# Division by the squared key length: from the keys of an RWKV-7 scan into the blocks of its inverse

## The chip, the cores and the metric

The kernel runs on one core of one Trainium2 chip. The metric is the device time of one execution in microseconds (us), as the median of several runs. A profile comes from one execution of its own, with its own time. The engines are called by their names in the profile: PE (TensorE, matrix products; PEld are its weight loads), DVE (VectorE), ACT (ScalarE), POOL (GpSimd), and SP (SyncE, which here issues the DMAs).

## The reference

The model is a trunk of two layers, with 1024 tokens, a width of 1024, and one final norm. Each layer normalizes its input, makes one combined projection, feeds three token mixers of width 512 (trailing means, retention, RWKV-7), gates and merges their outputs, and projects back. The change touches only the RWKV-7 mixer, which has 8 heads of 64 channels:

```
kk = heads(k * k_k)
kk = kk / max(sqrt(sum(kk * kk, axis=-1)), 1e-12)
k  = k * (1 + (a - 1) * k_a)
a_t, b_t = -kk, kk * a          # per head and token

def step(S, (r_t, w_t, k_t, v_t, a_t, b_t)):
    sa = einsum('bhvk,bhk->bhv', S, a_t)
    S  = S * w_t + sa (x) b_t + v_t (x) k_t
    return S, einsum('bhvk,bhk->bhv', S, r_t)
```

Both a_t and b_t carry the unit vector kk, and they only ever meet as a pair. One may therefore leave both of them unscaled and divide once, by the squared length of the key, anywhere on the way from sa to its use: it is one number for each token and head.

## The kernel before, in words

**The scan in chunks.** The tokens are cut into 16 chunks of 64. A head pair (two heads, 128 channels on 128 partitions) is worked on at a time, four pairs in a layer. Inside a chunk, the values sa of the 64 tokens depend on each other through a strictly triangular 64x64 matrix, so the kernel inverts (1 - triangle) for all 16 chunks and both heads at once, and then walks through the chunks with matrix products alone. For a head pair the steps are these:

- `prepare(h)` (line 1469), for each half h of 512 tokens: decay sums `Lc`, the squared keys `ksq`, split in two parts `ksh` and `ksl` so that a product with the block matrix `bone` sums them over a head's 64 channels in full precision (`nps`, lines 1490 to 1492). VectorE takes the maximum with 1e-24 (1494) and the reciprocal in two pieces of 256 (1495 to 1497): `rn` is one over the squared length, with the number of a token repeated on all 64 partitions of its head. Line 1507 multiplies key, k_k and rn, line 1509 multiplies with (a + 1), and lines 1518 to 1522 with the decay: `BK` holds the scaled b and k side by side.
- `place` (1541) writes the other operand, r and the unscaled key with their decay, into `AR`.
- `scores(q)` (1556): TensorE multiplies BK with AR for four chunks at a time, VectorE masks the products into `G`, which lies in the large tile `GX`.
- `invert()` (1603): of each 64x64 triangle, two 32x32 diagonal blocks are inverted on VectorE. A transpose brings them into `Lo` so that one partition holds one whole block in its 1024 elements, 64 partitions in all (two blocks, two heads, 16 chunks), and ScalarE copies `Lo` to `M` (1610). A recurrence of 30 steps follows (1614 to 1624), each of two VectorE instructions: an outer product of a column of Lo and a row of M into `RX`, and its sum into M. Line 1625 sets the diagonal to one. `back(b)` transposes block b into G, and `blocks` (1582) makes the off-diagonal block with 32x32 products on TensorE.
- `values(q)` (1641) prepares values, transposed keys (`BKt`) and the products `AV` that do not depend on the state.
- `main()` (1723): for each chunk, TensorE, VectorE (`xst`), TensorE (`ch`), ScalarE (`Z`), TensorE, VectorE (`S`, the new state) follow each other. Columns of the BKt tile beyond its 15 chunks hold `pc`, the decay over a chunk.

Pair hp + 1 is prepared, scored and inverted beside the scan of pair hp (`overlap`, `further`, lines 1795 to 1807). The pairs share the three slots of G (`SLOT`, 1438): the second half of a pair's scores waits for the first half of the chunks of the pair before.

**What fills TensorE beside it.** Large projections are made of 128x512 products in three passes (high and low halves of 32-bit numbers). A projection tile of 128 output channels takes 96 of them in the direct form (`in_tile2`, 2196). `SEQUENCE` (99) says which tiles are made in that form during a layer's scan: the k, r and v of head pairs 1 to 3, and a number g of branch gates in between. What is left comes afterwards in pairs, in a Strassen-like form that saves one product of eight (`forms`).

**What sets the order.** The program does not write an engine's order out by hand. A recorder (`Log`) collects all operations; `plan` (431) is a list scheduler that walks through modelled time with a cost for each instruction (`times`, 386), a cost and a landing time for each DMA, and a key for each operation (its place in the program and a bias of its lane), and sorts all five queues. Small two-operand subtractions on GpSimd may be moved to VectorE by it. Line 673 emits everything; it is therefore the line of almost every instruction in the profile, and groups are told apart by the names of their tiles. On the chip each queue then runs strictly in this order. A wait of the first instruction in a queue holds everything behind it.

Of the kernel before, what the change touches and what calls it, by code (L numbers as in the profile page):

```python
# [9 lines left out]
F32 = mybir.dt.float32  # L10
# [3 lines left out]
ALU = mybir.AluOpType  # L14
# [3 lines left out]
P = 128  # L18
D = 1024
T = 1024  # L20
L = 2
W = 512
HF = 512
# [72 lines left out]
COLUMNS = (1,)  # L96
TWICE = (1, 2)
SPARE = ((3, 2), (3, 3))
SEQUENCE = ('k1 r1 v1 g3 k2 r2 v2 g4 k3 g1 r3 v3 g12', 'k1 r1 v1 g3 k2 r2 v2 g4 k3 g1 r3 v3 g12')


ORDER = ("PE", "DVE", "ACT", "POOL", "SP")
# [584 lines left out]
def trunk_kernel(ctx, tc, xT, cvec, pos, vecs, consts, w_ada, w_all, pool_w, lora_w, out):  # L687
    nc = Log(tc.nc, tc)
# [125 lines left out]
    def vv(l, k, i):  # L814
        o = VEC[k] + i
        return vec[l][:, o : o + 1]
# [123 lines left out]
            yield 6000  # L940

    xd = [dp.tile([8, 2, P, HF], F32, name=f"xd{l}") for l in range(1)]
    gd = dp.tile([3, 8, 2, P, HF], F32, name="gd")
    hd = [dp.tile([8, 2, P, HF], F32, name=f"hd{l}") for l in range(L)]
    od = [dp.tile([3, 4, 2, P, HF], F32, name=f"od{l}") for l in range(L)]
# [75 lines left out]
    def pace(limit=900.0):  # L1021
        settle()
        return max(0.0, idle_at["DVE"] - clock[0] - limit)
# [416 lines left out]
    def rwkv_task(l, hp, kT, rT, vp, lt):  # L1440
# [12 lines left out]
        qa = lambda b: slice(64 + 32 * b, 96 + 32 * b)  # L1453
        BKt = BKt.rearrange("p (c n) -> p c n", n=P)
        Z = Z.rearrange("p (c n) -> p c n", n=P)
        pc = scan[l][1][:, 15 * P + 16 * hp : 15 * P + 16 * hp + 16]
        c3 = lambda t: t.rearrange("p (c t) -> p c t", t=CH)
        rm = cs("rmask", P).unsqueeze(1).to_broadcast([P, 4, P])
# [10 lines left out]
        def prepare(h):  # L1469
            if h == 0:  # L1470
                lw.append(lora_load(l, hp))
            yield wait(*lt[h])
            pss = [mx("lw"), mx("lw")]
            sg, aT = t_ri("sg"), t_ri("aT")
            lora_mm(pss, lw[0], lt[h], (sg, aT))
            nc.scalar.activation(sg, pss[0], AF.Tanh, bias=vv(l, "w0", hp), scale=0.5)
            yield 400
            nc.scalar.activation(aT, pss[1], AF.Tanh, bias=vv(l, "a0", hp), scale=0.5)
            sq = t_ri("ksq")
            nc.scalar.activation(sq, kT[h], AF.Square, scale=vv(l, "k_k", hp))  # L1480
            sqh = t_ri("ksh", F32R)
            nc.scalar.copy(sqh, sq)
            sql = t_ri("ksl", F32R)
            nc.vector.tensor_tensor(sql, sq, sqh.bitcast(F32), op=ALU.subtract)
            Lc = t_ri("Lc")
            nc.scalar.activation(sg, sg, AF.Identity, bias=ones)
            yield wait(sg)
            nc.vector.tensor_tensor_scan(Lc, same, sg, 0.0, op0=ALU.mult, op1=ALU.add)
            yield wait(sqh, sql, spare=1000)
            nps = mx("nps")  # L1490
            mmul(nps, bone, sqh, start=True, stop=False)
            mmul(nps, bone, sql, start=False, stop=True)
            rn = t_ri("rn")
            nc.vector.tensor_scalar_max(rn, nps, 1e-24)
            for j in range(2):
                yield pace()
                nc.vector.reciprocal(rn[:, 256 * j : 256 * j + 256], rn[:, 256 * j : 256 * j + 256])
            yield wait(Lc)
            Ep = sg
            nc.scalar.activation(Ep, Lc, AF.Exp, scale=-0.5 * KAPPA)  # L1500
            nc.scalar.activation(Lc, Lc, AF.Exp, scale=0.5 * KAPPA)
            Em = Lc
            kkn = rn
            ka = t_ri("ka")
            nc.scalar.activation(ka, aT, AF.Identity, bias=oka[l][:, hp : hp + 1], scale=vv(l, "k_a", hp))
            yield pace()
            nc.vector.scalar_tensor_tensor(kkn, kT[h], vv(l, "k_k", hp), rn, op0=ALU.mult, op1=ALU.mult)
            yield pace()
            nc.vector.scalar_tensor_tensor(kkn, aT, 1.0, kkn, op0=ALU.add, op1=ALU.mult)
            yield pace()  # L1510
            nc.vector.tensor_tensor(ka, ka, kT[h], op=ALU.mult)
            Ep_.append(Ep)
            for q in range(2):
                whole = t_ri("BK")
                b = whole.rearrange("p (c j t) -> p c j t", j=2, t=CH)
                part = slice(4 * q, 4 * q + 4)
                yield pace()
                nc.vector.scalar_tensor_tensor(
                    b[:, :, 0, :], c3(kkn)[:, part, :], -0.5, c3(Em)[:, part, :], op0=ALU.mult, op1=ALU.mult
                )  # L1520
                nc.vector.tensor_tensor(b[:, :, 1, :], c3(ka)[:, part, :], c3(Em)[:, part, :], op=ALU.mult)
                BK.append(whole)
            rk = ka
            yield pace()
            nc.vector.scalar_tensor_tensor(rk, rT[h], vv(l, "r_k", hp), ka, op0=ALU.mult, op1=ALU.mult)
            yield wait(rk)
            rkh = t_ri("rkh", F32R)
            nc.scalar.copy(rkh, rk)
            rkl = t_ri("rkl", F32R)
            nc.gpsimd.tensor_tensor(rkl, rk, rkh.bitcast(F32), op=ALU.subtract)  # L1530
            yield wait(rkh, rkl, spare=500)
            ps = mx("bon")
            bv = t_ri("bv")
            nc.touch(mmul(ps, bone, rkh, start=True, stop=False), bv)
            mmul(ps, bone, rkl, start=False, stop=True)
            nc.vector.scalar_tensor_tensor(bv, ps, 0.5, vp[h], op0=ALU.mult, op1=ALU.mult)
            bvs.append(bv)
            if h:
                prepared.add((l, hp))
# [36 lines left out]
        def back(b):  # L1576
            q = slice(32 * b, 32 * b + 32)
            src = M[q, :]
            src = src.rearrange("p (t s) -> p t s", s=32) if hi_ - lo_ == 1 else src.rearrange("p (t h s) -> p t h s", h=2, s=16)
            nc.vector.transpose(out=pair_(q, qa(b)), in_=src)  # L1580

        def blocks(*parts):
            tiles = [mx("m1") for _ in parts]
            with nc.together():
                for u in range(16):
                    for (i, q), ps in zip(parts, tiles):
                        rows = slice(32 - 32 * i, 64 - 32 * i)
                        w = 16 * q + u
                        g = 16 * (hi_ if q else lo_) + u
                        mmul(  # L1590
                            ps[rows, u * 32 : u * 32 + 32],
                            Lo[32:64, w * 32 : w * 32 + 32] if i else G[0:32, g, 96:128],
                            G[32:64, g, 96:128] if i else T13[:, w, :],
                            timed=True,
                        )
            for (i, q), ps in zip(parts, tiles):
                g = 16 * (hi_ if q else lo_)
                if i:
                    nc.scalar.copy(G[0:32, g : g + 16, 96:128], ps[0:32, :].rearrange("p (u s) -> p u s", s=32))
                else:  # L1600
                    nc.scalar.copy(Lo[32:64, q * HF : (q + 1) * HF], ps[32:64, :])

        def invert():
            for b in range(2):
                q = slice(32 * b, 32 * b + 32)
                yield pace()
                dst = Lo[q, :]
                dst = dst.rearrange("p (t s) -> p t s", s=32)
                nc.vector.transpose(out=dst, in_=pair_(q, qa(b)))
                nc.scalar.copy(M[q, :], Lo[q, :])  # L1610
            yield wait(MT)
            M3, L3 = (x.rearrange("p (t s) -> p t s", s=32) for x in (M, Lo))
            tm = RX[0:64, :]
            for i in range(1, 31):
                n = 31 - i
                pr = tm[:, 0 : n * i].rearrange("p (t s) -> p t s", s=i)
                nc.vector.tensor_tensor(
                    pr,
                    L3[:, i + 1 :, i : i + 1].to_broadcast([64, n, i]),
                    M3[:, i : i + 1, 0:i].to_broadcast([64, n, i]),  # L1620
                    op=ALU.mult,
                )
                nc.vector.tensor_tensor(M3[:, i + 1 :, 0:i], M3[:, i + 1 :, 0:i], pr, op=ALU.add)
                yield pace(600)
            nc.vector.memset(M[:, 0:1024:33], 1.0)
            nc.vector.transpose(
                out=T13.rearrange("p u s -> p s u"), in_=M[0:32, :].rearrange("p (t s) -> p s t", s=32)
            )
            yield pace()
            back(1)  # L1630
            yield pace()
            blocks((0, 0))
            yield 500
            back(0)
            yield 1500
            blocks((0, 1), (1, 0))
            yield 1500
            blocks((1, 1))
            yield wait(GX)

        def values(q):
# [1178 lines left out]
```

## Time and profile before

| | |
|---|---|
| median of 3 runs | 2245.52 us (2244.77 to 2245.91) |
| the profiled execution: its time, its span from first to last instruction | 2244.16 us, 2242.4 us |
| granted PE clock, mean | 0.997 |
| instructions of the program | 34866 |
| DMA | 247.79 MB, 111 GB/s on average |

An instruction group in the profile reads: line, engine, operation, tile written <- tiles read, shape and type, xcount, then busy us and mean ns, then the engine's idle time ahead of it, and what ended that. A tile row gives durations as min/median/max in ns, and the first and last start in us. A wait row gives who waited for whom, the total in us, how often, and the longest. Matmul records overlap, because TensorE takes up the next product before the last one has left.

The first layer's scan lies between about 190 and 546 us, the second layer's between about 1287 and 1631 us.

### The profile page before, as it was taken

To read this page: it belongs to the slowest core of one execution; us is meant where nothing else is said; L and a number is where in the kernel's file an instruction comes from. 1 tells how busy PE (TensorE), PEld (TensorE's weight loads), DVE (VectorE), ACT (ScalarE), POOL (GpSimd) and SP (SyncE) were. 2 spreads that over 40 slices of the span, in tenths; PEclk is the share of its full clock that TensorE was granted. 3 is DMA by queue.
4 is the path that set the end of the run, shared out by engine and by line. 5 is a ranking of instruction groups with operands and counts; after the bars stand their busy time and mean duration, and the time that the engine had idled before them with its cause. 6 is when DMAs were issued, how large, how long until landed. Compare 5 with 4: busy or idle time off the path is not lost.

```text
span 2242.4 us, 34866 instructions
## 1 busy us (share of the span) xinstructions
PE 2204.3 (98%) x12740; PEld 1823.8 (81%) x12740; DVE 1730.7 (77%) x2904; ACT 995.3 (44%) x1933; POOL 727.5 (32%) x629
## 2 busy tenths in 40 slices
PE   7999999999999999999999999999999999999998
PEld 6778888887888888888878887888888888888887
DVE  6888868886889886669787879799466767665895
ACT  5644554445333334324465354554443343341254
POOL 2222223233555663320042122232153455341100
PEclk9999999999999999999999999999999999999999
DMA  8111112333433335754451212133232122357343
GB/s 318 62 55 55 55 62 77 124 104 109 123 114 109 104 115 176 241 178 137 134 166 31 67 35 62 53 110 107 81 105 63 62 68 63 108 188 230 113 141 113
DMA packets 139195, 247.79 MB, mean 111 GB/s; under 512 B 15760, under 2 KB 21136, under 8 KB 139024
## 3 DMA queue, kind: packets, MB, share of 16 engines
q1 hardware_dynamic: 139024, 245.56, 34.7%
q8 instruction: 101, 1.65, 0.3%
q14 instruction: 70, 0.57, 0.1%
HBM read 185.99 MB, written 59.51 MB: 109 GB/s over the span
## 4 chain that ended last, share of the span: by engine, by line
PE 88%; DVE 6%; ACT 2%; DMA 1%; issue 1%; POOL 0%; SPq 0%; DVEq 0%; ACTq 0%; POOLq 0%
PE acc L673 73%; PE two L673 3%; PE ch L673 2%; PE g L673 1%; PE m L673 1%; PE ro L673 1%; PE av L673 1%; DVE rn L673 1%; DVE MT L673 1%; DVE RX L673 1%; PE pps L673 1%; PE rs L673 1%; PE bt L673 1%; PE lw L673 1%; PE rkv L673 0%
## 5 line engine op out<-in xcount | busy, mean ns | idle before, releaser
L673 PE MATMUL acc<-hlo,wh 128*128 128x512 f32 x1328 | 533.5, 402 | 0.0
L673 PE MATMUL acc<-hhi,wl 128*128 128x512 f32 x1328 | 532.7, 401 | 0.0
L673 PE MATMUL acc<-hhi,wh 128*128 128x512 f32 x1328 | 530.8, 400 | 0.5 <-DVE k L673 0.4
L673 POOL TENSOR_TENSOR wl<-wr,wh 128x512 fp32r<-128x512 f32 x125 | 170.4, 1364 | 404.3 <-ACT wh L673 170.0
L673 PEld LDWEIGHTS acc<-hhi,wh 128*128 128x128 f32 x1328 | 250.2, 188 | 45.9 <-DVE k L673 0.9
L673 PEld LDWEIGHTS acc<-hlo,wh 128*128 128x128 f32 x1328 | 250.3, 188 | 43.5
L673 PEld LDWEIGHTS acc<-hhi,wl 128*128 128x128 f32 x1328 | 250.3, 189 | 42.7
L673 PE MATMUL acc<-T,wh 128*128 128x512 f32 x768 | 244.4, 394 | 0.0
L673 ACT CAST wh<-wr 128x512 fp32r<-128x512 f32 x194 | 119.5, 616 | 198.5 <-PE acc L673 151.7
L673 POOL TENSOR_TENSOR wl<-wsum,wh 128x512 fp32r<-128x512 f32 x90 | 124.6, 1385 | 165.4 <-ACT wh L673 126.7
L673 PEld LDWEIGHTS acc<-T,wh 128*128 128x128 f32 x768 | 143.8, 188 | 29.7
L673 PE MATMUL acc<-T,wl 128*128 128x512 f32 x384 | 151.6, 395 | 0.0
L673 ACT CAST wh<-wsum 128x512 fp32r<-128x512 f32 x128 | 79.3, 620 | 140.6 <-PE acc L673 131.3
L673 ACT CAST wh<-wraw 128x512 fp32r<-128x512 f32 x108 | 66.9, 619 | 127.5 <-PE acc L673 79.2
L673 POOL TENSOR_TENSOR wl<-wraw,wh 128x512 fp32r<-128x512 f32 x59 | 85.5, 1450 | 72.8 <-ACT wh L673 66.2
L673 DVE SCALAR_TENSOR_TENSOR S<-ch,BKt,SP 64x64 f32<-64x64 f32 x224 | 63.3, 282 | 58.9 <-PE ch L673 55.8
L673 DVE TENSOR_TENSOR RX<-MT 64x30 f32<-64x30 f32 (+14 forms) x240 | 88.9, 370 | 8.6 <-ACT MT L673 1.3
L673 ACT ACTIVATE SP<-S,BKt 128x128 f32<-128x128 f32 x112 | 45.0, 402 | 104.4 <-DVE S L673 103.7
L673 DVE TENSOR_TENSOR MT<-MT,RX 64x30 f32<-64x30 f32 (+14 forms) x240 | 85.0, 354 | 7.3
L673 ACT ACTIVATE gsg<-acc 128x512 f32<-128x512 f32 x88 | 52.4, 595 | 80.3 <-PE acc L673 79.9
L673 ACT COPY Z<-ch 64x128 f32<-64x128 f32 x128 | 33.1, 259 | 120.5 <-PE ch L673 119.9
L673 PEld LDWEIGHTS acc<-T,wl 128*128 128x128 f32 x384 | 72.1, 188 | 14.8
(378 smaller groups left out, 5095.7 us busy)
## 6 DMA issues: line engine op xcount, KB each, us to landing
wr<-in_w_all SPq DMA_DIRECT2D x214, 256.0 KB, 2.7
wraw<-in_w_all SPq DMA_DIRECT2D x144, 256.0 KB, 2.7
gd<-gsg SPq DMA_DIRECT2D x96, 256.0 KB, 2.0
gs<-gd SPq DMA_DIRECT2D x84, 256.0 KB, 3.5
wada<-in_w_ada SPq DMA_DIRECT2D x80, 256.0 KB, 2.8
ol<-od SPq DMA_DIRECT2D x48, 256.0 KB, 3.3
traw<-hd SPq DMA_DIRECT2D x28, 256.0 KB, 3.0
x<-in_xT SPq DMA_DIRECT2D x16, 256.0 KB, 4.8
```

Source lines behind the costliest of these rows:

```text
L673: o.inst = f(*map(self.fixed, a), **{q: self.fixed(v) for q, v in k.items()})
```

## The change

In `prepare`, the maximum, the two reciprocals and the product with rn are gone from the keys. ScalarE copies nps out of PSUM (`ns`). SyncE stores two rows of it (one for each head) to DRAM, `nd`, and loads it back in another layout: `RN`, 64 partitions (block, head, chunk) by 32 tokens, in free columns of the BKt tile. The one remaining product, (a + 1) times the key, writes over `aT`. The factor k_k, which the program holds with its sign turned, goes into the product with the decay, in the place of the constant -0.5.

In `invert`, the transposed blocks go straight into M, and the recurrence reads and writes M alone. RN becomes 1 / (-2 max(n, 1e-24)), with n the squared length. One product over 64x1024 multiplies row t of each block with the number of token t ahead of the recurrence; another one multiplies column s with the number of token s behind it, after the diagonal has been set to one. The order of `back` and `blocks` at the end changes: block (0, 0) comes ahead of back(1), back(0) comes last.

In `SEQUENCE`, the gate between k3 and r3 moves to the end: g1 and g12 become g13, in both layers.

```diff
-SEQUENCE = ('k1 r1 v1 g3 k2 r2 v2 g4 k3 g1 r3 v3 g12', 'k1 r1 v1 g3 k2 r2 v2 g4 k3 g1 r3 v3 g12')
+SEQUENCE = ('k1 r1 v1 g3 k2 r2 v2 g4 k3 r3 v3 g13', 'k1 r1 v1 g3 k2 r2 v2 g4 k3 r3 v3 g13')
...
+    nd = [dp.tile([4, 2, 2, HF], F32, name=f"nd{l}") for l in range(L)]
...
+        RN = scan[l][1][0:64, 15 * P + 64 + 32 * (hp % 2) : 15 * P + 96 + 32 * (hp % 2)]
...
-            rn = t_ri("rn")
-            nc.vector.tensor_scalar_max(rn, nps, 1e-24)
-            for j in range(2):
-                yield pace()
-                nc.vector.reciprocal(rn[:, 256 * j : 256 * j + 256], rn[:, 256 * j : 256 * j + 256])
+            ns = t_ri("ns")
+            nc.scalar.copy(ns, nps)
+            nc.sync.dma_start(out=nd[l][hp, h], in_=ns[0:P:64, :])
+            for b in range(2):
+                o = 32 * b + 16 * (own[h] == hi_)
+                nc.sync.dma_start(
+                    out=RN[o : o + 16, :],
+                    in_=nd[l][hp, h].rearrange("e (c b t) -> (e c) b t", b=2, t=32)[:, b, :],
+                )
...
-            kkn = rn
+            kkn = aT
...
-            nc.vector.scalar_tensor_tensor(kkn, kT[h], vv(l, "k_k", hp), rn, op0=ALU.mult, op1=ALU.mult)
-            yield pace()
-            nc.vector.scalar_tensor_tensor(kkn, aT, 1.0, kkn, op0=ALU.add, op1=ALU.mult)
+            nc.vector.scalar_tensor_tensor(kkn, aT, 1.0, kT[h], op0=ALU.add, op1=ALU.mult)
...
-                    b[:, :, 0, :], c3(kkn)[:, part, :], -0.5, c3(Em)[:, part, :], op0=ALU.mult, op1=ALU.mult
+                    b[:, :, 0, :], c3(kkn)[:, part, :], vv(l, "k_k", hp), c3(Em)[:, part, :], op0=ALU.mult, op1=ALU.mult
...
-                dst = Lo[q, :]
+                dst = M[q, :]
                 dst = dst.rearrange("p (t s) -> p t s", s=32)
                 nc.vector.transpose(out=dst, in_=pair_(q, qa(b)))
-                nc.scalar.copy(M[q, :], Lo[q, :])
+            nc.vector.tensor_scalar(RN, RN, 1e-24, -2.0, op0=ALU.max, op1=ALU.mult)
+            nc.vector.reciprocal(RN, RN)
             yield wait(MT)
-            M3, L3 = (x.rearrange("p (t s) -> p t s", s=32) for x in (M, Lo))
+            M3 = M.rearrange("p (t s) -> p t s", s=32)
             tm = RX[0:64, :]
+            nc.vector.tensor_tensor(M3, M3, RN.unsqueeze(2).to_broadcast([64, 32, 32]), op=ALU.mult)
...
-                    L3[:, i + 1 :, i : i + 1].to_broadcast([64, n, i]),
+                    M3[:, i + 1 :, i : i + 1].to_broadcast([64, n, i]),
...
             nc.vector.memset(M[:, 0:1024:33], 1.0)
+            nc.vector.tensor_tensor(M3, M3, RN.unsqueeze(1).to_broadcast([64, 32, 32]), op=ALU.mult)
...
             yield pace()
+            blocks((0, 0))
             back(1)
-            yield pace()
-            blocks((0, 0))
+            yield 1000
+            blocks((0, 1), (1, 0))
             yield 500
+            blocks((1, 1))
             back(0)
-            yield 1500
-            blocks((0, 1), (1, 0))
-            yield 1500
-            blocks((1, 1))
             yield wait(GX)
```

## The prediction

> **What bounds the kernel now.** I read the page's engine lines first, then its chain of waits.
>
> ```profile
> PE 2204.3 (98%) x12740; PEld 1823.8 (81%) x12740; DVE 1730.7 (77%) x2904; ACT 995.3 (44%) x1933; POOL 727.5 (32%) x629
> ...
> PE 88%; DVE 6%; ACT 2%; DMA 1%; issue 1%; POOL 0%; SPq 0%; DVEq 0%; ACTq 0%; POOLq 0%
> ```
>
> TensorE is busy 98% of the span and carries 88% of the chain that ended last; VectorE, the engine that the change relieves, carries 6%. A busy share alone proves little here, because matmul records overlap. So I looked for a stretch in which TensorE waits for nothing, and at the stages of the scan beside it (busy time by stretch).
>
> ```profile
> 874.43 238.69 PE acc L673 x1040
> ...
> 150.00:250.00 100.00, 99.97 (x717) 82.73 (x715) 84.94 (x173) 50.62 (x111) 23.16 (x23) 1.00 0.17 53
> 350.00:450.00 100.00, 99.28 (x759) 81.20 (x757) 86.74 (x173) 47.36 (x109) 29.75 (x30) 1.00 0.33 103
> 875.00:1115.00 240.00, 240.00 (x1051) 196.59 (x1051) 176.36 (x244) 87.55 (x150) 45.68 (x32) 1.00 0.54 171
> ```
>
> The piece of the chain at 874 us is 1040 matmuls in 238.69 us, so one 128x512 matmul costs 0.2295 us when nothing holds it. The columns of the stretches are TensorE, weight loads, VectorE, ScalarE, GpSimd, clock and DMA. In the scan (150 to 250, 350 to 450) VectorE is busy 85% to 87%, yet TensorE is idle for at most 0.7 us in those 100. By weight loads, which do not overlap each other, the pure stretch stands at 196.59/240 = 81.9% and the whole span at 1823.8/2242.4 = 81.3%: what the program could still gain on TensorE, lead-in and end included, is some 0.7%, 16 us. The Trainium skill ("Perfetto Trace Analysis", Identifying the Most-Contended Engine) says that busy share is no measure for TensorE and that the share of weight loads should be used; the trace agrees, and adds that 82%, not 100%, is the ceiling here.
>
> What TensorE still waits for between 75 and 2200 us stands in the waits by engine (total us, times, longest):
>
> ```profile
> PE two L673 <- ACT y L673: 1.8, 1, 1.8
> PE acc L673 <- DVE r L673: 1.3, 1, 1.3
> PE two L673 <- DVE S L673: 1.2, 3, 0.6
> ...
> PE m L673 <- DVE MT L673: 0.9, 1, 0.9
> ...
> PEld ch L673 <- DVE xst L673: 7.4, 23, 0.5
> ```
>
> These are the waits that a lighter VectorE could shorten. The row on xst is the weight loads' idle time, most of which lies under a matmul that is still streaming; that is why it does not appear among TensorE's own waits.
>
> The last question is whether the scan's end sets the length of a layer's first stage. First and last starts of the gate evacuations and of the state update, first layer, then second:
>
> ```profile
> L673 ACT ACTIVATE gsg<-acc x40: 570/598/601, 154.5 to 562.5; 128x512 f32<-128x512 f32 x40
> ...
> L673 DVE SCALAR_TENSOR_TENSOR S<-ch,BKt,SP x112: 265/284/292, 194.8 to 545.1; 64x64 f32<-64x64 f32 x112
> ...
> L673 ACT ACTIVATE gsg<-acc x40: 577/598/602, 1253.5 to 1660.7; 128x512 f32<-128x512 f32 x40
> ...
> L673 DVE SCALAR_TENSOR_TENSOR S<-ch,BKt,SP x112: 265/284/292, 1292.0 to 1629.9; 64x64 f32<-64x64 f32 x112
> ```
>
> The state update ends 17.4 us and 30.8 us before the last gate. The recurrence is not late: TensorE's big products are. A scan that ends sooner buys nothing by itself.
>
> **The change, part by part.** *TensorE.* The matmuls are the same in number and shape. The sequence takes 3+4+1+12 = 20 gates now and 3+4+13 = 20 after, so as many go through the direct products and as many through the paired ones. On the path: 0.
>
> *VectorE, preparation.* Sixteen halves (2 layers, 4 head pairs, 2 halves) each lose the maximum from PSUM, two reciprocals and one product.
>
> ```profile
> L673 DVE RECIPROCAL rn<-rn 128x256 f32<-128x256 f32 x32 | 55.6, 1742 | 0.5
> L673 DVE SCALAR_TENSOR_TENSOR rn<-k,vec,rn 128x512 f32<-128x512 f32 x16 | 11.6, 726 | 0.2
> L673 DVE TENSOR_SCALAR rn<-nps 128x512 f32<-128x512 f32 x16 | 10.9, 680 | 0.8 <-PE nps L673 0.6
> L673 DVE TENSOR_TENSOR mlo<-mrg,mhi 128x512 fp32r<-128x512 f32 x32 | 21.9, 684 | 0.0
> L673 DVE TENSOR_TENSOR BK<-ka,Lc 128x256 f32<-128x256 f32 x32 | 13.4, 418 | 0.2
> L673 DVE STREAM_TRANSPOSE GX<-MT 32x1024 f32<-32x1024 f32 x16 | 31.1, 1946 | 0.4
> ...
> L673 DVE RECIPROCAL rn<-rn x37: 165/1752/1754, 17.3 to 2234.9; 128x256 f32<-128x256 f32 x32, 128x4 f32<-128x4 f32 x3, 128x2 f32<-128x2 f32 x2
> ```
>
> Removed: 55.6 + 11.6 + 10.9 = 78.1 us, or 4.9 us a half. The product that is left now writes over aT, so it waits for ScalarE's read of aT; behind it stands only the product with ka, which needs that same ScalarE result, so this costs nothing.
>
> *VectorE, inverse.* Eight inverses each gain two products of 64x1024, a maximum and a reciprocal of 64x32. A product grows from 418 ns at 256 to 684 at 512, 1.04 ns an element, so 1024 cost 684 + 532 = 1.22 us. The trace has no 64x1024 product; its bounds are 0.68 (the 512 row, if a broadcast operand were free) and 1.37 (twice that row). The reciprocal lies between 0.165 (4 elements) and 1.742 (256), on their line at 0.34; the small maximum I put at 0.2. Together 2 x 1.22 + 0.54 = 3.0 us an inverse, 24 us in all. Net VectorE: -54 us of 1730.7, nearly all in the scan stages.
>
> *ScalarE.* It loses the copy of the transposed block and gains a copy out of PSUM.
>
> ```profile
> L673 ACT COPY MT<-MT 32x1024 f32<-32x1024 f32 x16 | 16.8, 1047 | 14.6 <-DVE MT L673 14.4
> ...
> L673 ACT COPY s<-acc 128x512 f32<-128x512 f32 x64 | 37.3, 582 | 10.0 <-PE acc L673 10.0
> ```
>
> That is -16.8 + 16 x 0.582 = -7.5 us on an engine at 44%. The PSUM bank of nps is now freed by ScalarE after 0.58 us instead of by VectorE after 0.68.
>
> *The chain of the inverse.* Gone is one ScalarE copy of 1.05 us ahead of the recurrence and the step back(1), a transpose of 1.95 us, ahead of the first block product; new are the 3.0 us. It is as long as before, within a microsecond either way. The blocks' products and back(0) only change order.
>
> *The DMAs and SyncE's queue.* Each half stores 4 KB and loads two pieces of 2 KB: 48 new issues. The loads must see the store's landing, and SyncE stands meanwhile.
>
> ```profile
> gd<-gsg SPq DMA_DIRECT2D x96, 256.0 KB, 2.0
> ...
> lraw<-in_lora_w SPq DMA_DIRECT2D x16, 64.0 KB, 2.1
> ...
> fixed<-in_cvec SPq DMA_DIRECT2D x1, 4.0 KB, 1.7
> ...
> SPq L673 <- POOL wl L673: 473.3, 120, 38.7
> ...
> SPq L673 <- DMA od<-wo: 22.2, 8, 3.9
> ...
> L673 DVE TENSOR_SCALAR rn<-nps x16: 659/679/692, 88.2 to 1489.0; 128x512 f32<-128x512 f32 x16
> ...
> L673 DVE MEMSET MT<- x8: 85/85/85, 150.8 to 1532.6; 64x32 f32 x8
> ```
>
> The number a token needs is there 0.6 (copy) + 2.0 (store) + 1.7 to 2.1 (load) = 4.3 to 4.7 us after nps. In the last head pair nps is read at 1489.0 and the recurrence begins by 1532.6: 43.6 us of cover, of which the shorter preparation may take 10. What queues behind the waiting SyncE are the weight loads; a store followed by its load holds it 22.2/8 = 2.8 us in the program now, so 16 times that is 45 us, spread over both scans. SyncE stands 473 us for the weight halves' buffers anyway. I take 0; without that cover it would be up to 2.8 us a time. The Trainium skill speaks against this step ("DMA: Bandwidth & Descriptors", Two DMAs through the same engine are not ordered): the issuing engine must wait for the first DMA's semaphore before it issues the second. The row on od shows just such a wait, 2.8 us on average.
>
> *The sequence.* One gate, 96 x 0.2295 = 22.0 us of TensorE, moves from before r3 to after v3. The last pair's preparation starts 22 us earlier, beside the scan of pair 2, and the gate lands where nothing else waits. On the path: 0, unless the collision below happens.
>
> **The sum.** What is left for TensorE to gain are waits. At least none go (0); at most the rows r, S, MT and the weight loads on xst all go, 1.3 + 1.2 + 0.9 + 7.4 = 10.8 us. I take TensorE's own rows, 3.4 us, because they are time in which nothing streamed. ScalarE's 1.8 stays: nothing in the change touches it. New waits can cost as much as old ones, so the end on the other side is +3.4. The profiled execution took 2244.16 us, 1.8 around a span of 2242.4; 2244.16 - 3.4 = 2240.8. The median of the runs lies 1.36 above that execution, so 2242 us.
>
> **The rivals.** *More comes free than the waits show* (2230 to 2237, say 2233): entering and leaving small matmuls also costs TensorE, and a calmer VectorE lets the planner group them better. The 16 us worked out above are the limit. Against it: lead-in and end are in those 16 us, and the number of scan steps stays.
>
> *The freed time is filled again* (2244 to 2247): the planner orders every queue anew by its own cost model and may move GpSimd subtractions to VectorE, so that the waits return at other places. For it: today's few waits are scattered, no step of the scan is systematically late.
>
> *The early preparation collides with the scan* (2250 to 2258, say 2254, slower). The moved gate brings pair 3's preparation into pair 2's scan, where VectorE was 87% busy, and one step shows what a burst in its queue does:
>
> ```profile
> 416.26 2.99 DVE L673 TENSOR_TENSOR traw<-traw,traw 128x512 f32<-128x512 f32 x3 [0.16 <-DMA traw<-hd]
> ...
> 419.89 0.46 PE L673 MATMUL two<-S,CX 128*128 128x128 f32 x2 [0.61 <-DVE S L673]
> ```
>
> Three subtractions ahead of S, and TensorE, whose order is fixed, stands for 0.61 us. Pairs 2 and 3 have 15 such steps each, in two layers 60. With 14 more of them late by 0.61 us the result is 8.5 us above my forecast, 2250.5; that is the point from which it decides, and 20 give 2254. Against it: the preparation is 4.9 us a half lighter.
>
> *The number comes late.* Should a weight load ahead of the store hold SyncE for its longest, 38.7 us, the 4.7 us no longer fit into 43.6 - 10, and VectorE stands at the head of the inverse: (38.7 + 4.7 - 33.6) = 9.8 us once, 2252 us.
>
> **How the numbers follow.** A measurement of this kernel can tell about 0.2% (4.5 us) from no change: below 2241.0 is faster, above 2250.0 slower. My forecast, 2237 to 2246, has 0.60, of which 0.24 lies below 2241. The gain beyond the waits has 0.13, the refilling 0.14, the collision 0.10, the late number 0.03. Faster: 0.24 + 0.13 = 0.37. Same: 0.36 + 0.14 = 0.50. Slower: 0.13. The range is 2235 to 2251: it takes in the forecast, the refilling, a third of the first rival and the edge of the collision. The forecast's own range is 2237 to 2246.
>
> **What would show it.** Right: VectorE busy near 1676 us, ScalarE near 988, TensorE's instructions still 12740 and its share still 98%; recurrence products no shorter; the first rows of the waits on S, MT and r smaller, none new above 2 us. The last state update should come before 545 us and 1630 us with the last gate where it was. A row "DVE RN <- DMA" of more than a microsecond would prove the late number, waits on S in steps of pairs 2 and 3 the collision. The forecast is wrong if the span moves by more than the waits add up to.

## The result, and the profile after

The changed kernel takes 2239.93 us, median of 11 runs (2238.61 to 2241.09), against 2245.07 us (2243.57 to 2246.70) for 11 runs of the kernel before on the same chip: ratio 0.9974 [0.9966, 0.9982], 5.1 us less. The forecast was 2242.0 us, 3.5 below the median it started from. The profiled execution after took 2240.18 us with a span of 2238.4, 4.0 less than before.

The page's engine lines and the shares of its chain, after:

```profile
PE 2200.3 (98%) x12740; PEld 1824.4 (82%) x12740; DVE 1676.6 (75%) x2877; ACT 980.6 (44%) x1931; POOL 720.0 (32%) x624
...
PE 85%; DVE 9%; ACT 2%; issue 1%; DMA 1%; POOL 1%; SPq 0%; DVEq 0%; POOLq 0%; ACTq 0%
```

VectorE lost 54.1 us of work, and the span lost 4.0. TensorE has the same 12740 matmuls, and it is idle for as long as before: 2242.4 - 2204.3 = 38.1 us then, 2238.4 - 2200.3 = 38.1 us now. So all of the 4.0 us have gone out of the time in which TensorE counts as busy; the same products stand closer together. VectorE's share of the chain rose from 6% to 9% while it works less: the chain is one path among several, and a share that moves by three points is no measure of what bounds.

The waits by engine between 75 and 2200 us, after:

```profile
PE two L673 <- DVE S L673: 1.6, 3, 1.1
PE pps L673 <- ACT pdh L673: 1.1, 2, 0.8
...
PE acc L673 <- DVE r L673: 0.6, 1, 0.6
...
PEld ch L673 <- DVE xst L673: 4.3, 14, 0.5
```

The rows on y (1.8) and MT (0.9) are gone, r went from 1.3 to 0.6, xst from 7.4 (23 times) to 4.3 (14 times). S rose from 1.2 to 1.6 and pps from 0.7 to 1.1. All listed rows of TensorE's own waits add up to 10.4 us before and 9.2 after.

The stage ends, first layer and then second (gate evacuations, state update), and the start of the second layer (ssps, first start):

```profile
L673 ACT ACTIVATE gsg<-acc x40: 577/598/603, 151.7 to 559.8; 128x512 f32<-128x512 f32 x40
...
L673 DVE SCALAR_TENSOR_TENSOR S<-ch,BKt,SP x112: 267/284/292, 181.5 to 540.9; 64x64 f32<-64x64 f32 x112
...
L673 PE MATMUL ssps<-fixed,ssum x32: 164/250/250, 1111.0 to 2228.2; 128*128 128x1 f32 x32
...
L673 ACT ACTIVATE gsg<-acc x40: 575/598/604, 1249.0 to 1654.4; 128x512 f32<-128x512 f32 x40
...
L673 DVE SCALAR_TENSOR_TENSOR S<-ch,BKt,SP x112: 267/284/292, 1277.5 to 1621.4; 64x64 f32<-64x64 f32 x112
```

The same row on ssps before:

```profile
L673 PE MATMUL ssps<-fixed,ssum x32: 164/250/250, 1113.0 to 2232.2; 128*128 128x1 f32 x32
```

So the span splits into four stages, here as in the table further down: to the last gate of layer 1 (562.5 before, 559.8 after), from there to ssps, the paired products (550.5, 551.2), from ssps to the last gate of layer 2 (547.7, 543.4), and the rest (581.7, 584.0). The two scan stages gave 2.7 + 4.3 = 7.0 us, the other two took 0.7 + 2.3 = 3.0 back. Inside the first, TensorE's idle time went from 21.4 to 22.4 us, inside the third from 5.0 to 3.0: in the first layer none of the gain is idle time, in the second about half.

Where in the scan stages? Busy time by stretch, before and then after (columns as in the prediction: TensorE, weight loads, VectorE, ScalarE, GpSimd, clock, DMA):

```profile
90.00:280.00 190.00, 189.11 (x1268) 155.22 (x1267) 165.11 (x312) 95.18 (x199) 45.62 (x49) 1.00 0.16 48
280.00:565.00 285.00, 281.99 (x2117) 232.20 (x2115) 223.63 (x447) 142.67 (x320) 88.41 (x79) 1.00 0.31 98
...
1200.00:1390.00 190.00, 188.59 (x1371) 154.59 (x1369) 163.65 (x308) 93.26 (x192) 40.74 (x43) 1.00 0.17 52
1390.00:1660.00 270.00, 268.99 (x1953) 222.35 (x1953) 195.34 (x393) 127.80 (x295) 86.98 (x79) 1.00 0.29 92
```

```profile
90.00:280.00 190.00, 188.87 (x1377) 154.44 (x1376) 150.55 (x303) 95.62 (x205) 46.23 (x50) 1.00 0.16 48
280.00:565.00 285.00, 282.41 (x2014) 234.62 (x2013) 211.04 (x440) 135.35 (x312) 88.00 (x80) 1.00 0.31 98
...
1200.00:1390.00 190.00, 188.44 (x1410) 154.06 (x1409) 154.12 (x310) 90.91 (x198) 44.19 (x47) 1.00 0.17 52
1390.00:1660.00 270.00, 269.83 (x1926) 225.73 (x1925) 181.52 (x379) 121.51 (x287) 73.07 (x69) 1.00 0.30 93
```

The second number, the weight loads, says more about the work done than the first, for the loads of the 128x512 products stand apart (0.19 us each, one every 0.23). It is not exact: loads of small products do overlap in the records (in the kernel before two of 0.19 us begin at 402.48 and 402.59). And the stretches of one layer cannot be read singly, because the scan now starts earlier (first S at 181.5 instead of 194.8) and some hundred small products have moved from the later stretch into the earlier one (1268 and 2117 matmuls before, 1377 and 2014 after). The sums over a layer rose from 387.4 to 389.1 us and from 376.9 to 379.8. Of these, the first rise is hardly more than the other pause gives the kernel before (388.6, see below), and the second is still larger in the kernel that has VectorE's load back (380.7). VectorE is 9 to 15 us less busy in each of the four stretches. TensorE's own busy time shows hardly any of this.

### The profile page after: what moved, and what is told of

The parts are those of the page before. It is cut to its first block, busy times and chain, and to the rows that moved or that the text cites. A ratio compares the mean times of both kernels' runs of the same rounds, so it can differ in the third digit from the quotient of the medians.

```text
span 2238.4 us, 34921 instructions
## 1 busy us (share of the span) xinstructions
PE 2200.3 (98%) x12740; PEld 1824.4 (82%) x12740; DVE 1676.6 (75%) x2877; ACT 980.6 (44%) x1931; POOL 720.0 (32%) x624
## 4 chain that ended last, share of the span: by engine, by line
PE 85%; DVE 9%; ACT 2%; issue 1%; DMA 1%; POOL 1%; SPq 0%; DVEq 0%; POOLq 0%; ACTq 0%
PE acc L673 71%; PE two L673 3%; PE ch L673 2%; DVE MT L673 2%; PE g L673 2%; PE av L673 1%; DVE RX L673 1%; PE ro L673 1%; PE m L673 1%; PE rs L673 1%; DVE GX L673 1%; PE bt L673 1%; PE pps L673 1%; DVE S L673 0%; PE lw L673 0%
## 5 line engine op out<-in xcount | busy, mean ns | idle before, releaser
L673 POOL TENSOR_TENSOR wl<-wr,wh 128x512 fp32r<-128x512 f32 x118 | 162.2, 1376 | 328.0 <-ACT wh L673 135.3
```

Of the source, the lines that this page charges most:

```text
L673: o.inst = f(*map(self.fixed, a), **{q: self.fixed(v) for q, v in k.items()})
```

## The experiments

The change has three parts that can be undone one at a time: the **load** (what left VectorE's queue), the **sequence** (one gate moved), and the **end of the inverse** (the order of back and blocks). The rival to all of them is that any new plan of the queues, with nothing of substance changed, moves the time as much. Each ratio is to the kernel before, timed on the same chip; its median there was 2244.0 to 2245.4 us, so kernels timed on different chips are compared by their ratios.

### Re-planning alone

The planner adds a pause, MARGIN, before each TensorE instruction that uses another engine's result. A slightly different pause gives a new order of the same work. In the kernel before and in the changed one:

```
-MARGIN = 300
+MARGIN = 310
```

> The kernel before with one planner constant changed that means nothing here (300 to 310 ns of margin ahead of TensorE). It does the same work in another order, so it shows what a mere rearrangement of the queues is worth. If the change's 5 us are more than that: within 2 us of before, 0.999 to 1.001. If rearranging alone gives and takes 5 us: outside 0.9985 to 1.0015.

> The changed kernel with the same planner constant changed (300 to 310 ns). If the gain belongs to the change: 0.9965 to 0.9985. If it belonged to one lucky order: 0.999 to 1.001, like after_old_sequence.

Measured: 1.0003 [0.9994, 1.0012] and 0.9983 [0.9974, 0.9992]. A new plan alone moved the kernel before by 0.03%, the changed one by 0.09%, 2 us. Two more pairs below, each with both pauses, differ by 0.01%. A single plan is therefore good to about 0.1%; the change's 0.26% is more than that, and still there (0.17%) under the other pause.

### The load, taken out of the kernel before

In the kernel before, in both sequences, the two reciprocals are left out and the maximum carries a constant factor in their place:

```
-            nc.vector.tensor_scalar_max(rn, nps, 1e-24)
-            for j in range(2):
-                yield pace()
-                nc.vector.reciprocal(rn[:, 256 * j : 256 * j + 256], rn[:, 256 * j : 256 * j + 256])
+            nc.vector.tensor_scalar(rn, nps, 1e-24, 1e-7, op0=ALU.max, op1=ALU.mult)
```

> The kernel before without the reciprocals (the maximum is scaled by 1e-7 instead, so that the division by the squared length is left out); everything else stays, VectorE is 56 us lighter. Theory A: ratio 0.997 to 0.999, without RN, without DMAs and without the new sequence. Theory B, and the view that the rearranged inverse matters: 0.999 to 1.001.

> The kernel before without its reciprocals (division left out, as in before_no_reciprocal) and with the new sequence. If the moved gate pays only when VectorE is light, 0.995 to 0.997, some 3 us below before_no_reciprocal (0.998). If the sequences differ by no more than any rearrangement of the queues does, 0.997 to 0.999.

Measured: 2239.53 us, 0.9981 [0.9973, 0.9990], and with the new sequence 2241.30 us, 0.9982 [0.9973, 0.9991]. VectorE is busy 1686.1 us in the first, close to the 1676.6 of the changed kernel. These two kernels leave out the division by the squared length; they serve for the time alone. Taking VectorE's load away, with nothing else of the change, gives 0.19%, and the sequence adds nothing to it. But the keys also get rid of the wait for the reciprocals here, so this pair alone cannot tell a lighter queue from a shorter chain.

### The load, put back into the changed kernel

The first try wrote the dummy maximum, reciprocals and product into a tile of its own:

```
+            dm = t_ri("dm")
+            nc.vector.tensor_scalar_max(dm, ns, 1e-24)
+            for j in range(2):
+                yield pace()
+                nc.vector.reciprocal(dm[:, 256 * j : 256 * j + 256], dm[:, 256 * j : 256 * j + 256])
+            yield pace()
+            nc.vector.scalar_tensor_tensor(dm, kT[h], vv(l, "k_k", hp), dm, op0=ALU.mult, op1=ALU.mult)
```

> The changed kernel with VectorE's old load put back as work that nobody reads: a maximum, two reciprocals of 128x256 and a product of 128x512 in each half, 4.9 us a half, on a copy in SBUF; keys and inverse stay as changed. Theory A in its form 'the load on VectorE's queue': the gain goes, ratio 0.999 to 1.001. Theory A in its form 'the keys no longer wait for the reciprocals': the gain stays, 0.997 to 0.998.

Measured: 2275.51 us, 1.0137 [1.0122, 1.0153]. That is far more than the load, for VectorE's 1755.5 us are only 25 above the kernel before. The tile takes a slot of a pool, and that is another change. The stage rows of the first layer say what it did:

```profile
L673 ACT ACTIVATE gsg<-acc x40: 580/598/602, 157.0 to 555.7; 128x512 f32<-128x512 f32 x40
...
L673 DVE SCALAR_TENSOR_TENSOR S<-ch,BKt,SP x112: 265/284/292, 200.4 to 580.1; 64x64 f32<-64x64 f32 x112
```

The state update ends 24.4 us after the last gate, where it ended 17.4 us ahead of it in the kernel before: the scan's last steps have no big products beside them. The timeline of TensorE there, and the stretch of 10 us around it:

```profile
569.57 0.46 PE L673 MATMUL two<-S,AR 128*128 128x128 f32 x2 [0.76 <-DVE S L673]
570.41 0.70 PE L673 MATMUL ch<-xst,GX 128*65 128x64 f32 x4 [0.38 <-DVE xst L673]
570.90 0.65 PE L673 MATMUL two<-Z,GX 128*65 128x64 f32 x4
571.46 0.80 PE L673 MATMUL ch<-Z,BKt 128*128 128x128 f32 x2
573.02 0.77 PE L673 MATMUL two<-S,AR 128*128 128x128 f32 x2 [0.76 <-DVE S L673]
...
576.79 0.77 PE L673 MATMUL two<-S,AR 128*128 128x128 f32 x2 [0.77 <-DVE S L673]
```

```profile
570.00:580.00 10.00, 7.11 (x35) 5.38 (x34) 2.88 (x9) 2.35 (x8) 0.20 (x1) 0.51 0.05 19
```

A bare step takes 576.79 - 573.02 = 3.77 us, and the granted clock falls to 0.51. This kernel tells what an uncovered end of the scan costs; it does not tell the price of the load. So the load was put back again, over `ns`, without a new buffer, and under both pauses:

```
+            nc.vector.tensor_scalar_max(ns, ns, 1e-24)
+            for j in range(2):
+                yield pace()
+                nc.vector.reciprocal(ns[:, 256 * j : 256 * j + 256], ns[:, 256 * j : 256 * j + 256])
+            yield pace()
+            nc.vector.scalar_tensor_tensor(ns, kT[h], vv(l, "k_k", hp), ns, op0=ALU.mult, op1=ALU.mult)
```

> As after_load_back, but the work that nobody reads is written over ns once its two rows are stored, so that no buffer more is held than in the kernel before. Load theory (VectorE's queue is what makes TensorE wait): ratio to before 0.999 to 1.002. Theory that the 31 us of after_load_back came from the extra buffer: at least 25 us less than there. Theory that only the waiting of the keys for the reciprocals counted: 0.997 to 0.998, as the change itself.

> after_load_in_place in the order that a margin of 310 ns gives. Load theory: both scan stages stay 2 to 5 us longer than in the changed kernel, whatever the stage of paired products does; ratio 0.998 to 1.001. Theory that VectorE's load plays no part and only the shorter chain of the keys counts: scan stages as in the changed kernel, within 1 us, ratio 0.996 to 0.998.

Measured: 2248.02 us, 1.0010 [1.0001, 1.0019], and 2248.18 us, 1.0011 [1.0002, 1.0019]. With the load back the whole gain is gone, in both plans. But the stage table below puts most of the loss (5.7 of 5.8 us in the span) into the paired products of the first layer, behind the scan. Of the 7.0 us of the scan stages 4.7 are kept, under the other pause 3.1 of 8.0. For the second run it was expected that both scan stages would be 2 to 5 us longer than in the changed kernel; they are 3.8 and 1.1 longer. The scan itself does run later (its last state update at 550.2 instead of 540.9 us), but as its end is still covered, that stage is only 0.9 us longer. TensorE's waits between 565 and 875 us begin with

```profile
PE pps L673 <- ACT pdh L673: 2.5, 3, 2.1
PE adaps L673 <- DVE ada_acc L673: 1.9, 1, 1.9
```

where the changed kernel has 1.1 for the first and nothing above 0.5 for the second. The longest of each come one after the other in TensorE's timeline. Behind them stands the stretch of 20 us around them, in this kernel and then in the changed one:

```profile
838.04 1.02 PE L673 MATMUL adaps<-fixed,ada_acc 128*128 128x1 f32 x8 [1.86 <-DVE ada_acc L673]
...
842.56 0.80 PE L673 MATMUL pps<-pdh,pw 128*128 128x512 f32 x1 [2.06 <-ACT pdh L673]
```

```profile
830.00:850.00 20.00, 16.08 (x77) 12.97 (x77) 18.53 (x24) 5.44 (x9) 12.13 (x9) 0.83 0.48 146
```

```profile
830.00:850.00 20.00, 18.86 (x102) 14.97 (x100) 18.00 (x28) 7.86 (x14) 8.47 (x6) 1.00 0.46 133
```

The granted clock is 0.83 over these 20 us where the changed kernel has 1.00; that is about 20 x 0.17 = 3.4 us of lost clock. Over the whole stage TensorE is idle for 6.25 us against 2.84, 3.4 more. The two together, 6.8 us by this estimate, cover the 5.7 that the stage lost.

### The sequence

The new one in the kernel before; the old one in the changed kernel, under both pauses:

```
-SEQUENCE = ('... k3 g1 r3 v3 g12', '... k3 g1 r3 v3 g12')
+SEQUENCE = ('... k3 r3 v3 g13', '... k3 r3 v3 g13')
```

> The kernel before with the new sequence alone (g13 at the end). Theory A: no gain, ratio 0.999 to 1.001, as the scan's end is not what sets the stage. Theory B: ratio 0.997 to 0.998. The rival of the prediction in which the earlier preparation collides with the scan of pair 2: with VectorE as full as before it should show most clearly here, 1.002 or more.

> The changed kernel with the old sequence (the gate g1 back between k3 and r3). Theory A, a lighter VectorE is what shortens TensorE's waits: the gain of 5 us stays, ratio to before 0.997 to 0.999. Theory B, the moved gate brings it: ratio 0.999 to 1.001, and the last gate of each first stage back near 562 and 1660 us.

> The changed kernel with the old sequence, in the other order of the queues that a margin of 310 ns gives. If the old sequence itself costs the changed kernel its gain: 1.000 to 1.002, as in after_old_sequence. If that was the draw of one order, in a stage that the change does not touch (the paired products of the first layer, where it lost 7 us): 0.997 to 0.999.

Measured: in the kernel before 2242.64 us, 0.9995 [0.9986, 1.0003]; the changed kernel with the old sequence 2246.09 us, 1.0010 [1.0001, 1.0019], and 2248.15 us, 1.0011 [1.0002, 1.0020]. By itself the sequence is worth nothing. In the changed kernel, taking it back costs the whole gain, 0.36%. The gate that moves is 11 us of TensorE, not 22: `in_tile2` issues 48 products for a tile, not 96, and the last two gates of the changed kernel, with the scan over, are evacuated 11.4 us apart (1640.31 and 1651.68).

### The end of the inverse

The old order of back and blocks, with the pauses that went with it, in the changed kernel:

```
-            blocks((0, 0))
             back(1)
-            yield 1000
-            blocks((0, 1), (1, 0))
+            yield pace()
+            blocks((0, 0))
             yield 500
-            blocks((1, 1))
             back(0)
+            yield 1500
+            blocks((0, 1), (1, 0))
+            yield 1500
+            blocks((1, 1))
```

> The changed kernel with the old order at the end of the inverse (back(1), block (0,0), back(0), the other blocks). The prediction put this part at nothing: ratio to before 0.996 to 0.999, within 2 us of the changed kernel. If taking back(1) off the way of the first block pays: 0.999 to 1.001, and more waiting of m for MT.

Measured: 2247.38 us, 1.0012 [1.0003, 1.0021], more than either expectation allowed for; it was timed in one plan only. The copies of the finished blocks into G for pair 1, in this kernel and then in the changed one, and this kernel's stage rows of the first layer:

```profile
L673 ACT COPY GX<-m x2: 574/574/575, 299.5 to 301.1; 32x512 f32<-32x512 f32 x2
```

```profile
L673 ACT COPY GX<-m x2: 578/578/578, 270.8 to 272.5; 32x512 f32<-32x512 f32 x2
```

```profile
L673 ACT ACTIVATE gsg<-acc x40: 576/598/602, 152.0 to 552.7; 128x512 f32<-128x512 f32 x40
...
L673 DVE SCALAR_TENSOR_TENSOR S<-ch,BKt,SP x112: 266/284/292, 183.9 to 564.2; 64x64 f32<-64x64 f32 x112
```

The blocks of pair 1 come 28.7 us later (in the kernel before, with the same old order, they came at 283.6), the scan runs late, and its end stands 11.5 us behind the last gate, bare. The paired products' stage takes 568.2 us in place of 551.2, of which the earlier last gate gives 7.1 back: ssps starts 9.9 us later. With 24.4 us bare (the extra tile) it started 30.0 later.

### Fewer gates in the second layer

Since the second layer's scan ends 33 us ahead of its last gate, part of the gates can go from the direct products into the paired ones, which saves 12 big products. The changed kernel with, for the second layer only:

```
-'k1 r1 v1 g3 k2 r2 v2 g4 k3 r3 v3 g13'
+'k1 r1 v1 g3 k2 r2 v2 g4 k3 r3 v3 g11'
```

> The changed kernel with two gates of the second layer moved from the direct products to the paired ones (g11 instead of g13): 12 products of 0.23 us less, 2.75 us. If the scan, which now ends 33 us before the last gate of that stage, may lose that cover: ratio to before 0.995 to 0.997. If the end of the scan then lies bare (two gates are 44 us): 0.998 to 1.003, with TensorE waiting for S and xst around 1610 us.

Measured: 2235.73 us (5 runs), 0.9961 [0.9949, 0.9974], with 12728 matmuls. Twelve big products are 12 x 0.2295 = 2.75 us; the ratios differ by 0.13%, 2.9 us, little more than a new plan moves, and their intervals overlap at their ends. The two gates are 22 us and not the 44 of the expectation: the stage from ssps to the last gate is 521.2 us here and 543.4 in the changed kernel. The scan keeps 10.9 us of cover.

### The stages side by side

Worked from the same rows of every kernel's trace (us; one profiled execution each; the runs of one kernel lie 2.5 to 8.7 us apart, so the ratio of all its runs stands beside it):

| kernel | to last gate, 1 | paired, 1 | ssps to last gate, 2 | rest | span | ratio |
|---|---|---|---|---|---|---|
| before | 562.5 | 550.5 | 547.7 | 581.7 | 2242.4 | 1 |
| before, other pause | 563.1 | 553.0 | 547.3 | 582.6 | 2246.0 | 1.0003 |
| before, new sequence | 562.3 | 549.7 | 545.0 | 582.9 | 2239.9 | 0.9995 |
| before, no reciprocals | 562.1 | 555.3 | 543.0 | 582.3 | 2242.7 | 0.9981 |
| the same, new sequence | 560.8 | 550.4 | 544.9 | 583.4 | 2239.5 | 0.9982 |
| after | 559.8 | 551.2 | 543.4 | 584.0 | 2238.4 | 0.9974 |
| after, other pause | 559.7 | 551.7 | 542.7 | 582.6 | 2236.7 | 0.9983 |
| load back in place | 560.7 | 556.9 | 544.8 | 581.8 | 2244.2 | 1.0010 |
| the same, other pause | 563.5 | 556.8 | 543.8 | 582.9 | 2247.0 | 1.0011 |
| old sequence | 561.3 | 554.5 | 543.9 | 581.5 | 2241.2 | 1.0010 |
| the same, other pause | 564.5 | 557.0 | 543.8 | 582.3 | 2247.6 | 1.0011 |
| old end | 552.7 | 568.2 | 542.6 | 581.7 | 2245.2 | 1.0012 |

(The profiled execution of "before, no reciprocals" was the slowest of its 11, 2244.76 us where the median is 2239.53.) Two things are to be seen. The second layer's scan stage is 3 to 5 us shorter in every kernel with any part of the change, also in the two that have VectorE's old load back; its gain is never lost again. What the kernels at 1.001 lose, they lose in the first layer: 3 to 6 us in its paired products where the scan's end is covered, 17 where it is not, and under the other pause 4 to 5 us in its scan stage as well.

What the paired products lose can be made out by the estimate used above, more idle time of TensorE in that stage plus lost clock. Against the changed kernel under the same pause, the load back under the other pause has 3.0 + 1.7 = 4.7 us (5.1 measured), the old sequence 2.8 + 0 (3.3 measured), the old sequence under the other pause 0.9 + 3.4 = 4.3 (5.3 measured). The profiled execution of "before, no reciprocals" has 3.2 + 1.7 = 4.9 more than the kernel before (4.8 measured): a clock of 0.83 between 840 and 850 us is there too.

## Why the prediction was right, and where it was not

**What bounds: right.** 54 us off VectorE gave 5 us, because TensorE's products carry the time. The test for it is the kernel with the load back in place: its scan ended 9.3 us later under cover and made the first stage only 0.9 us longer.

**The waits, -3.4: about the right size, but not from the waits.** The forecast took TensorE's own rows "because they are time in which nothing streamed". That time did not shrink: 38.1 us idle before, 38.1 after, and the listed own rows fell by 1.2 us, not 3.4 (MT, half of r and the unforeseen y went; S, pps and others grew). The span's 4.0 us came out of busy time. Some of it may be the weight loads' idle time (xst, 3.1 us less), which lies mostly under a streaming matmul and which the forecast had set aside; the rows cannot say how much. The mechanism that the first rival named, small products costing TensorE less on their way in and out, fits better than the forecast's own; no run isolates it. Nor did the sum hold anything for the stages behind the scans, where 3.0 of 7.0 us were lost again. That the number came close is in good part luck. By the forecast's own sign, a span that moves by more than the waits add up to, its account fails for TensorE's own rows (4.0 against 1.2). The weight loads that were said not to overlap do so among small products, so the 16 us worked out from them are a rough limit.

The last gate was forecast "where it was" and came 2.7 and 6.3 us earlier: with TensorE's products setting the stage, that is what a gain has to look like, and the test was put badly.

"ScalarE's 1.8 stays: nothing in the change touches it" failed. The stall on y lay behind two loads of ScalarE's function tables in the kernel before:

```profile
520.87 1.28 ACT L673 ACT_TABLE_LOAD   x1
522.16 0.63 ACT L673 ACTIVATE nrot<-nrot 64x512 f32<-64x512 f32 x1
522.82 1.28 ACT L673 ACT_TABLE_LOAD   x1
524.11 0.60 ACT L673 ACTIVATE gsg<-acc 128x512 f32<-128x512 f32 x1
524.60 0.61 ACT L673 CAST wh<-wr 128x512 fp32r<-128x512 f32 x1
525.11 0.26 ACT L673 COPY y<-two 64x128 f32<-64x128 f32 x1
```

The new plan put that activation elsewhere; there are 8 table loads after, 10 before. A stall that comes from where a plan happens to lay something is not a fixed term.

**VectorE, -54 to 1676: right.** The operations that were added:

```profile
L673 DVE TENSOR_TENSOR MT<-MT,BKt 64x1024 f32<-64x1024 f32 x16 | 20.2, 1264 | 0.5
...
L673 DVE RECIPROCAL BKt<-BKt 64x32 f32<-64x32 f32 x8 | 2.8, 344 | 0.2
...
L673 DVE TENSOR_SCALAR BKt<-BKt 64x32 f32<-64x32 f32 x8 | 1.5, 185 | 0.1
```

1.26, 0.34 and 0.19 us against 1.22, 0.34 and 0.2: 24.5 us in all, and -78.1 + 24.5 = -53.6.

**ScalarE, 988: 980.6.** The copies came as forecast (16.8 us gone, 16 of 0.58 new). Another 2 x 1.28 us are the two table loads; no other group's busy time moved by more than 0.3 us, so most of the remaining 4.7 is how the records overlap.

**The inverse as long as before, blocks and back worth 0: the second half failed.** "The blocks' products and back(0) only change order" left out that the next pair's scan waits for these blocks. With the old order they come 28.7 us later in pair 1 and the scan's end loses its cover. The statement that the recurrence is not late, and that a scan which ends sooner buys nothing, holds as long as the cover of 17.4 us holds; I did not give the price beyond it. That price, the later start of ssps, is some 10 us for 11.5 us bare and 30 us for 24.4 us bare. Each is one execution of one kernel, and the second also carries the load and the extra tile.

**The number through DRAM: right, for the reason given.** For the last pair's second half ScalarE copied nps at 1474.74; SyncE, then VectorE, followed:

```profile
1475.33 0.48 SPq L673 DMA_DIRECT2D nd<-ns  x1
1476.93 0.83 SPq L673 DMA_DIRECT2D BKt<-nd  x2
```

```profile
1481.89 0.17 DVE L673 TENSOR_SCALAR BKt<-BKt 64x32 f32<-64x32 f32 x1
...
1518.38 1.22 DVE L673 TENSOR_TENSOR MT<-MT,BKt 64x1024 f32<-64x1024 f32 x1
```

The number is first read by the maximum (TENSOR_SCALAR), 7.2 us after the copy and 5.0 after the loads were issued. As VectorE's order is fixed, this is the cover that counts, and it was enough. The first product that needs the number runs 43.6 us after the copy; the forecast had 43.6 less up to 10. No engine waits for RN anywhere. What SyncE stands for, after:

```profile
SPq L673 <- POOL wl L673: 397.8, 111, 16.4
...
SPq L673 <- ACT ns L673: 73.0, 14, 11.1
...
SPq L673 <- DMA nd<-ns: 7.9, 11, 1.1
```

The forecast gave SyncE 45 us for the landings. They cost 7.9 (0.7 each, not 2.8), but it had left out that SyncE also stands for ScalarE's copy, 73.0 us. The sum is almost twice the forecast, and it cost nothing visible, since SyncE stood 75.5 us less for the weight halves' buffers. SyncE's wait between store and load shows here too: the load's issue came 1.60 us after the store's.

**The sequence, 0: right alone, wrong in company.** The gate was counted at 96 products and 22.0 us; it is 48 products and 11.0 us. In the kernel before it is worth 0.05% with 1 inside the interval, with the reciprocals gone 0.01%. In the changed kernel its absence costs 0.36%. The step that failed is to add the parts up: load, sequence and end of the inverse are not independent. Any one of them taken back gives 1.001, and each loses half of it or more in the first layer's paired products, which the change does not touch.

**The rivals.** The late number and the collision did not come: no wait on RN, and no more than 1.6 us of waits on S. The refilling did not come in the full change; something like it came in each kernel with one part undone, where the scan stages' gain is lost in the first layer's paired products. What they lose there is TensorE idle time on pdh, ada_acc and their neighbours, and in four of the five a granted clock that falls with it; why each plan puts these waits there **stays open**, for no run changed that stage by itself. "More comes free than the waits show" came short of its price (5.1 us in the median against some 12), but its mechanism fits the unchanged idle time better than the forecast's.

**What is shown, what is argued.** Shown: without the reciprocals the kernel before gains 0.19% [0.10, 0.27], by a lighter VectorE, by keys that come sooner, or by both. Shown: with the load back the change gains nothing in the whole. Not shown: that the load is what shortens the scan stages, since they keep 4.7 of 7.0 us (3.1 of 8.0) with it. Shown in one plan, with order and pauses changed together: the early blocks keep the scan covered. Not settled: where TensorE's 4.0 us of busy time went, and how the sequence, by one gate, decides over the gain once the rest is there.

## What to carry to other kernels

Where one engine is busy all the time, a lighter second engine does not pay by its own microseconds. Before you forecast a gain by the first engine's waits, plan to compare its idle time (span less busy time) before and after: if that does not move, the gain has come from somewhere else, however well the number fits. Read the granted clock beside every stretch of waits; here two waits of some 2 us close together cost nearly as much again in clock. Before you call a step's order free, find what starts when it ends and how much cover that has: here 17 us of big products hid the scan's end, and beyond them a bare microsecond cost about one (0.9 and 1.2 in the two cases). Where a planner orders everything anew, first time an edit that changes nothing but the plan (here up to 0.1%), and undo the parts one by one; they may not add up.

## What was not expected of the hardware

- With the scan bare, TensorE's granted clock fell to 0.51 between 570 and 580 us (the row is above), though its records fill 7.11 of those 10 us; a pair of 128x128 products took 0.77 us in place of 0.46. The Trainium skill ("TensorE: Matmul & The Clock Gate", Part 1: The HAM clock gate) gives half the clock to a TensorE that was idle over a window of about 3.4 us. The trace agrees with the half; it adds that steps with gaps of no more than 0.8 us each were enough.
- In the paired products, with big products on both sides, two waits of 1.86 and 2.06 us within 7 us went with a granted clock of 0.50 between 840 and 845 us (load back in place). Other plans with waits there show 0.83 over 10 us, and the changed kernel under the other pause, with one wait of 2.3 us, no fall at all.
- A store of 4 KB followed by a load of 2 KB took 1.60 us from one issue to the other, and the loads landed 1.6 us after their issue by the page's median, both below the 1.7 to 2.1 us of the rows that the forecast went by (4 to 256 KB).
- A ScalarE table load costs 1.28 us; two of them around one activation stood ahead of a copy that TensorE needed (the rows of 520 to 525 us above).
